# Feed-forward products of 512 columns over both operand parts, and later landings in the planner

## The chip, the cores and the metric

The kernel runs on one core of a Trainium2 chip. The metric is the device time of one execution in microseconds (us), the median of several runs. The profile and the trace are of one further execution, taken by the hardware profiler.

## The reference

The input x is 256 tokens of 1024 channels. Two blocks follow each other. The first has one recurrent mixer with a dilated attention and one feed-forward; the second has two layers, each of feed-forward, sparse-attention mixer and feed-forward, so there are five feed-forwards in all. Each of the eight sub-layers is conditioned: a vector c goes through `silu(c) @ w_ada`, which gives a shift, a scale and a gate of 1024 channels each. Cut to what matters here:

```python
def swiglu(h, w13, w2):                      # w13: 1024 x 5632, w2: 2816 x 1024
    a, b = jnp.split(h @ w13, 2, axis=-1)
    return (jax.nn.silu(a) * b) @ w2

h = rms_norm(x, g) * (1 + scale) + shift
x = x + 0.5 * gate * swiglu(h, w13, w2)
```

All values are float32, and the result is compared as float32.

## The kernel before

Activations are kept transposed, channels on the 128 partitions and the 256 tokens along the free dimension (`S` = 256), as chunks of 128 x 256. A product is one matmul with a 128 x 128 piece of the weights as stationary operand and one activation chunk as moving operand, so the output chunk is 128 x 256 and lies in PSUM.

**Two parts of each number.** TensorE takes the operands from tiles of type `fp32r`. Each operand is split into a high part (the value copied into such a tile) and a low part (the value less that copy), and `mm3` makes three products for each pair of chunks: high weights by high operand, high weights by low operand, low weights by high operand, all summed in the same PSUM region. For the weights, `load_split` loads 512 KB into a tile `raw` (128 x 1024, four row chunks of a pair of column chunks), ACT writes `hi` and DVE writes `lo` = raw - hi. For the activations the same is done once for a chunk: `hh` and `hl` are the parts of the normalised input, `fh` and `fl` (or `fg`) those of the gated hidden values.

**The feed-forward** (`ffn`) has 22 units (`NF`). A unit takes one column chunk of the left half of w13 and the matching one of the right half, 8 row chunks each. The first three units run on the input before its normalisation is known (`pair_u`, 258 columns, banks "a" and "b"). The other 19 use `pair`: both column chunks lie in one PSUM bank of the name "mm", the first in columns 0 to 255, the second in columns 256 to 511, and two such banks take turns. Then ACT makes `su` = silu of the first, DVE makes `fy` = second times `su`, and `split` makes the parts. The output product (`out_proj`) runs over 22 row chunks in four pairs of column chunks; the last pair has a bank for each chunk so that the end comes earlier. Below, the 19 units are called a feed-forward's first half, the output product its second half.

**Conditioning.** `_ada_unit` loads a row block of w_ada (`raw<-in_ada`, 128 x 1024) and reduces it against c in one DVE instruction, whose discarded full-size output is the tile `junk`. `load_split` starts such a block after a part of the weight loads (`rate` 0.55 for each load), until all are done; the results are needed sub-layers later.

**The order.** Every stretch of the kernel is recorded first: each call makes an `_Op` with an engine, a cost and a lag, and the overlaps of tiles make the edges (`_Stretch.add`, `edge`). `emit` then solves a list schedule by these costs, tries several, and issues each engine's instructions in the order of the best one; an engine works through its own in that order. All instructions have the line L725 in the profile, since one helper issues them, so they are told apart by the tiles' names. The planner's cost of a load is

```python
            if self.name == "dma":
                return rec.add(_Op("dma", emit, n / 360e3, 0.0), [out], src)
```

with no lag beyond a fixed 0.95 us from a load to the engine that reads it (`LAG`).

Of the kernel before, what the change touches and what calls it, by code (L numbers as in the profile page):

```python
# [12 lines left out]
F32 = mybir.dt.float32  # L13
# [13 lines left out]
S = 256  # L27
# [4 lines left out]
SHIFT = 2560  # L32
HP = HS = 0
EXPM05 = float(np.exp(np.float64(-0.5)))

# [580 lines left out]
class _Model:  # L618


    def __init__(self):
        self.at = {"pe": 0.0, "dve": 0.0, "act": 0.0, "pool": 0.0, "dma": 0.0}
        self.uses, self.slots = {}, {}
        self.rec = None
# [54 lines left out]
class _Engine:  # L679
# [42 lines left out]
    def record(self, op, f, a, k):  # L722
        rec = self.model.rec
        aps = [x for x in (*a, *(v for n, v in k.items() if n != "accum_out")) if _is_ap(x)]
        emit = lambda: f(*a, **k)  # L725
        if op == "dma_start":
            out = aps[0]
            src = [aps[1]] if aps[1].space == SBUF else []
            n = out.nbytes() if callable(out.nbytes) else out.nbytes
            if self.name == "dma":  # L730
                return rec.add(_Op("dma", emit, n / 360e3, 0.0), [out], src)
            return rec.add(_Op(self.name, emit, 0.06, 2.2 + n / 360e3), [out], src)
        if not aps:
            return rec.add(_Op(self.name, emit, 1.28, 0.0), [], [])
        outs = [aps[0]] + ([k["accum_out"]] if k.get("accum_out") is not None else [])
        ins = aps[1:]
        x = _Op(self.name, emit, self.time(op, aps[0], ins, k), 0.0)
        if self.name == "pe":

            x.sums = k.get("start") is False  # L740
            rows, cols = ins[0].ap[0][1], aps[0].ap[0][1]
            at = lambda a: a.offset // a.ap[0][0] // 32
            x.cols = ins[1].free_size() * rows * cols / 16384.0 * \
                (1 if ins[1].dtype == F32R else 2 if k.get("is_transpose") else 4)
            x.pas = 1 if ins[1].dtype == F32R or k.get("is_transpose") else 2
            x.d = x.hold = x.cost / x.pas
            size = lambda n: 32 if n <= 32 else 64 if n <= 64 else 128
            x.mode = size(rows), size(cols)
            if x.mode != (128, 128):
                r0, c0 = at(ins[0]), at(aps[0])  # L750
                x.subs = tuple(4 * r + c for r in range(r0, r0 + x.mode[0] // 32) for c in range(c0, c0 + x.mode[1] // 32))
                x.hold = (x.pas - 1) * x.d + 0.007
            else:
                x.hold = x.cost
        elif self.name in ("dve", "pool"):
            x.port = sum(1 for a in ins if a.space == SBUF and a.free_size() > 1) > (self.name == "dve")
        return rec.add(x, outs, ins)
# [30 lines left out]
class _Kernel:  # L788
# [90 lines left out]
    def vec(self, name, j=0, n=None):  # L879
        o, w = self.vat[name]  # L880
        return self.vect[:, o + j:o + (w if n is None else j + n)]

    def split(self, y, hi, lo):

        self.act(hi, y)
        self.tt(lo, y, hi.bitcast(F32), SUB)
# [134 lines left out]

    def mm3(self, out, wh, wl, xh, xl, first, last):
        self.mm(out, wh, xh, first, False)
        self.mm(out, wh, xl, False, False)
        self.mm(out, wl, xh, False, last)

    def pair(self, nk, H, L, tag="mm", last=False):

# [137 lines left out]

    def scaled(self, sub, pool, tag):

        self.G = [self.t(pool, [128, S], tag % j) for j in range(KC)]
        for j, g in enumerate(self.G):  # L1170
            self.act(g, self.x[j], AF.Copy, scale=self.mod(sub)[:, 8 + j:9 + j])

# [2 lines left out]
        self.chunk_hl(self.G[j], self.mod(sub), j, j >= 8)  # L1175

    def chunk_hl(self, n, m, j, pool=False):
        h = self.t(self.hp, [128, S], "hh%d" % j, F32R)
        l = self.t(self.hp, [128, S], "hl%d" % j, F32R)
        ins = self.act(h, n, AF.Identity, bias=m[:, j:j + 1])  # L1180
        if pool:
            self.nc.gpsimd.tensor_scalar(n, n, 1.0, m[:, j:j + 1], MUL, ADD)
            self.ptt(l, n, h.bitcast(F32), SUB)
        else:
            self.stt(l, n, m[:, j:j + 1], h.bitcast(F32), ADD, SUB)
        self.H.append(h)
        self.L.append(l)
        return ins
# [16 lines left out]
        while self.bg:  # L1205
            self.bg.popleft()()

    def out_proj(self, nk, H, L, sub, fpool=None):


        nc = self.nc
        m = self.mod(sub)
        nxt = sub + 1 if sub + 1 < self.n_sub else None
        if nxt is not None:
            self.operand_u(nxt)
        self.new_sum()
        f = []

        def update(j, src):
            if src is not None:  # L1220
                self.stt(self.x[j], src, m[:, 16 + j:17 + j], self.x[j], MUL, ADD)
            rec = self.model.rec
            if nxt is not None:
                rec.late = -40 / 10
                self.chunk_u(nxt, j)
            rec.late = 40 / 10
            self.add_square(self.x[j], j, KC - 4 if fpool is not None else KC - 2)
            rec.late = 0.0

        for p in range(4):  # L1230
            ps = self.pair(nk, H, L, last=p == 3)
            for c in range(2):
                j = 2 * p + c
                pc = ps[c] if p == 3 else ps[:, c * S:c * S + S]
                if fpool is None:
                    update(j, pc)
                else:
                    t = self.t(fpool, [128, S], "f%d" % j)
                    self.add_square(pc, j)
                    self.act(t, pc, AF.Copy, scale=m[:, 16 + j:17 + j])  # L1240
                    f.append(t)
        if fpool is not None:
            r = self.rstd(self.sums)
            self.behind_r = self.r_ins
            self.keep_warm(14, H[0], self.sums)
            self.new_sum()
            for j in range(KC):
                self.tt(f[j], f[j], r, MUL)
                self.tt(self.x[j], f[j], self.x[j], ADD)
                update(j, None)  # L1250


    def ffn(self, sub, n):
        tc, nc = self.tc, self.nc
        n_u = 3
        with ExitStack() as rx:
            fp, ft = (self.pool(rx, "ffn%d%d" % (n, b), b) for b in (1, 2))
            hh, hl = [], []
            pend = []

            def gated(k, y):
                h = self.t(fp, [128, S], "fh%d" % k, F32R)
                l = self.t(fp, [128, S], "fl%d" % k if k < NF - KC else "fg%d" % (k - NF + KC), F32R)
                self.split(y, h, l)
                hh.append(h)
                hl.append(l)

# [27 lines left out]
            for k in range(n_u, NF):  # L1295
                if sub == 2 and k == 8:
                    self.rope2_tables(self.pool(rx, "rt2"))
                ps = self.pair(KC, self.H, self.L)
                su = self.t(ft, [128, S], "su")
                self.act(su, ps[:, :S], AF.Silu)  # L1300
                y = self.t(ft, [128, S], "fy")
                self.tt(y, ps[:, S:], su, MUL)
                gated(k, y)
            self.use_table(LNEXP)
            self.out_proj(NF, hh, hl, sub, fp if sub < 2 else None)
            self.emit(sub + 3, rx)


    def weave(self, streams, dense=None, share=0.0):
# [82 lines left out]
    def token_loads(self, w, H, L, views, post):  # L1392
# [5 lines left out]
        def quantum(k, q):  # L1398
            def f(hi, lo):
                if k == 0:  # L1400
                    box.extend(self.psum("mm") for _ in range(2))
                ws = slice(q * w, q * w + w)
                for x, (xh, xl) in enumerate(zip(views(H[k]), views(L[k]))):
                    pv = box[x][:, :w]
                    self.mm(pv, xh, hi[:, ws], k == 0, False)
                    self.mm(pv, xl, hi[:, ws], False, False)
                    self.mm(pv, xh, lo[:, ws], False, k == KC - 1)
# [9 lines left out]
    def start(self, late):  # L1417
# [15 lines left out]
        for k in range(KC):  # L1433
# [3 lines left out]
            self.act(gs, gs, AF.Identity, scale=self.vec("g0", k, 1), bias=b1[:, k:k + 1])  # L1437
            self.act(shift, shift, AF.Identity, bias=self.vec("b0", k, 1))
            self.act(xr[k], xr[k], AF.Identity, scale=gs, bias=shift)
            h = self.t(self.hp, [128, S], "hh%d" % k, F32R)  # L1440
            l = self.t(self.hp, [128, S], "hl%d" % k, F32R)
            ins = self.act(h, xr[k])
            self.tt(l, xr[k], h.bitcast(F32), SUB)
            self.H.append(h)
            self.L.append(l)
            while k >= 6 and late:
# [18 lines left out]
    def mixer1(self, sub):  # L1465
        tc, nc, vec = self.tc, self.nc, self.vec
        with ExitStack() as cx:
# [178 lines left out]
            for n in range(4):  # L1646
                psa = self.pair(6, zh, zl)
                psb = self.pair(2, oh, ol, "a").rearrange("p (a b) -> p a b", a=2)
                for c in range(2):
# [7 lines left out]
                            psb[:, c].rearrange("p (r i) -> p i r", r=2),  # L1657
                            s2[:, 1].rearrange("p (i r) -> p i r", r=2), MUL)
                    self.tt(a1, a1, b1, ADD)
                    h = self.t(self.hp, [128, S], "hh%d" % j, F32R)  # L1660
                    l = self.t(self.hp, [128, S], "hl%d" % j, F32R)
                    self.split(a1, h, l)
                    mH.append(h)
                    mL.append(l)
            self.use_table(LNEXP)
# [511 lines left out]
    def mixer2(self, sub, l):  # L2177
        nc = self.nc
        c2 = self.c2
        with ExitStack() as cx:  # L2180
# [139 lines left out]
            oH, oL = [None] * 8, [None] * 8  # L2320

            def finished(n, po):
                oH[n] = self.t(p1, [128, S], "oh%d" % n, F32R)
                oL[n] = self.t(p1, [128, S], "ol%d" % n, F32R)
                self.act(oH[n], po[:, :S])
                self.tt(oL[n], po[:, :S], oH[n].bitcast(F32), SUB)

            def nsa(j, bank):
                gt = res["gt"]
# [138 lines left out]
```

## Time and profile before

| | |
|---|---|
| median of 3 runs | 1653.19 us |
| lowest and highest | 1648.75 and 1653.45 us |
| the profiled execution's own time | 1650.98 us |
| its span, first to last instruction | 1648.9 us |
| mean granted TensorE clock over the span | 0.992 |
| busy share of the span: PE, DVE, ACT | 96%, 75%, 58% |
| read from HBM | 356.25 MB |

PE is TensorE's matmuls, PEld its weight loads, DVE is VectorE, ACT is ScalarE, SP is SyncE, which issues all loads. Busy time is the union of an engine's instructions, and a matmul's end is modelled, so the spacing between the starts of matmuls says more than their durations. The span is the profiled execution's; 2.1 us of its own time lie around it.

### The profile page before, as it was taken

How to read it: one execution, taken by the hardware profiler on the slowest of the kernel's cores; microseconds unless marked ns; L12 is line 12 of the kernel's file. 1: busy time of each engine (PE TensorE's matmuls, PEld its weight loads, DVE VectorE, ACT ScalarE, POOL GpSimd, SP SyncE). 2: the span in 40 equal slices, each digit the busy share in tenths (PEclk: the TensorE clock that was granted, in tenths of full speed). 3: DMA queues.
4: the chain of work that ended last, by engine and by line, in shares of the span. 5: the costliest groups of instructions: out<-in, count | busy, mean ns of one | idle time of the engine just before them, and what ended most of it. 6: DMA issues, size and time to landing. Idle time of an engine off the chain costs nothing. (4 is left out here: it accounts for less than half of the span.)

```text
span 1648.9 us, 35735 instructions
## 1 busy us (share of the span) xinstructions
PE 1581.3 (96%) x14250; PEld 1495.3 (91%) x14250; DVE 1234.8 (75%) x2547; ACT 962.2 (58%) x1851; POOL 18.5 (1%) x39
## 2 busy tenths in 40 slices
PE   4999999989999899999999999999999999999998
PEld 4988888889999899999788999999999978899997
DVE  6897775687777797787869877778768887875544
ACT  5674554767444474445697744456454569874542
POOL 0010000000000000000000000000000000000001
PEclk9999999989999999999999999999999999999999
DMA  9645354465888858888524588876888753255552
GB/s 363 254 141 195 101 182 147 134 220 181 292 290 290 285 199 299 281 298 280 173 92 145 184 294 296 277 278 214 300 274 302 278 170 116 82 168 198 182 174 95
DMA packets 102696, 359.64 MB, mean 218 GB/s; under 512 B 11392, under 2 KB 13056, under 8 KB 102528
## 3 DMA queue, kind: packets, MB, share of 16 engines
q1 hardware_dynamic: 102528, 357.34, 63.6%
q8 instruction: 112, 1.84, 0.5%
q14 instruction: 56, 0.46, 0.1%
HBM read 356.25 MB, written 1.05 MB: 217 GB/s over the span
## 5 line engine op out<-in xcount | busy, mean ns | idle before, releaser
L725 DVE TENSOR_TENSOR lo<-raw,hi 128x1024 fp32r<-128x1024 f32 (+2 forms) x478 | 556.3, 1184 | 187.4 <-issue 75.9
L725 ACT ACTIVATE hi<-raw 128x1024 fp32r<-128x1024 f32 (+2 forms) x478 | 486.8, 1026 | 350.7 <-PE ps_mm L725 254.4
L725 PE MATMUL ps_mm<-hh,hi 128*128 128x256 f32 x2040 | 510.0, 286 | 19.2 <-ACT hh L725 9.2
L725 PE MATMUL ps_mm<-hl,hi 128*128 128x256 f32 x2040 | 505.2, 285 | 0.0
L725 PEld LDWEIGHTS ps_mm<-hh,hi 128*128 128x128 f32 x2040 | 387.4, 192 | 27.7 <-DVE fy L725 12.0
L725 PEld LDWEIGHTS ps_mm<-hl,hi 128*128 128x128 f32 x2040 | 387.2, 192 | 2.0 <-issue 0.8
L725 PE MATMUL ps_mm<-hh,lo 128*128 128x256 f32 x2040 | 316.7, 286 | 0.0
L725 DVE CUSTOM_DVE_ANT_0 junk<-raw,cond 128x1024 bf16<-128x1024 f32 x192 | 235.6, 1227 | 64.0 <-DMA raw<-in_ada 63.3
L725 PEld LDWEIGHTS ps_mm<-hh,lo 128*128 128x128 f32 x2040 | 275.7, 193 | 2.9 <-issue 1.1
L725 PE MATMUL ps_mm<-fh,hi 128*128 128x256 f32 x770 | 188.9, 281 | 0.0
L725 PEld LDWEIGHTS ps_mm<-fh,hi 128*128 128x128 f32 x770 | 144.5, 188 | 0.9 <-DVE fy L725 0.9
L725 PE MATMUL ps_mm<-fl,hi 128*128 128x256 f32 x490 | 120.4, 280 | 0.0
L725 PE MATMUL ps_mm<-fh,lo 128*128 128x256 f32 x770 | 115.5, 281 | 2.5 <-DVE lo L725 2.5
L725 PEld LDWEIGHTS ps_mm<-fh,lo 128*128 128x128 f32 x770 | 102.0, 188 | 2.8 <-DVE lo L725 2.8
L725 ACT ACTIVATE fh<-fy 128x256 fp32r<-128x256 f32 x110 | 44.9, 412 | 94.1 <-DVE fy L725 94.1
L725 PEld LDWEIGHTS ps_mm<-fl,hi 128*128 128x128 f32 x490 | 92.2, 188 | 0.0
L725 PE MATMUL ps_mm<-fg,hi 128*128 128x256 f32 x280 | 69.4, 281 | 0.0
L725 PE MATMUL ps_a<-UH,hi 128*128 128x258 f32 x168 | 49.4, 297 | 6.1 <-ACT UH L725 6.1
L725 PEld LDWEIGHTS ps_mm<-fg,hi 128*128 128x128 f32 x280 | 52.7, 188 | 0.0
L725 ACT ACTIVATE su<-ps_mm 128x256 f32<-128x256 f32 x95 | 35.6, 375 | 29.0 <-PE ps_mm L725 28.9
L725 ACT ACTIVATE UH<-x,mod 128x256 fp32r<-128x256 f32 x56 | 26.4, 501 | 43.6 <-DVE x L725 43.6
L725 PE MATMUL ps_a<-UL,hi 128*128 128x258 f32 x168 | 48.9, 293 | 0.0
(559 smaller groups left out, 2631.3 us busy)
## 6 DMA issues: line engine op xcount, KB each, us to landing
raw<-in_ffi SPq DMA_DIRECT2D x220, 512.0 KB, 5.4
raw<-in_ada SPq DMA_DIRECT2D x192, 512.0 KB, 5.3
raw<-in_ffo SPq DMA_DIRECT2D x100, 512.0 KB, 5.1
raw<-in_win SPq DMA_DIRECT2D x66, 512.0 KB, 4.3
raw<-in_wout SPq DMA_DIRECT2D x24, 512.0 KB, 4.1
w<-in_cw SPq DMA_DIRECT2D x16, 512.0 KB, 8.0
raw<-in_ws SPq DMA_DIRECT2D x16, 448.0 KB, 7.5
raw<-in_ffo SPq DMA_DIRECT2D x20, 256.0 KB, 4.0
```

The source lines that it names most:

```text
L725: emit = lambda: f(*a, **k)
```

## The change

Three things change in the feed-forwards. First, the high and low parts of an activation chunk share one tile of 128 x 2 x 256, high part first. `parts` makes it and returns the high part and the whole tile; `low` picks the low part out of a whole tile. Second, `pair_wide` replaces `pair` in the 19 units and in three of the four output pairs: one product of 512 columns multiplies the high weights by both parts of the operand into a bank of its own, and one of 256 columns adds low weights by high part to the bank's first half. The two column chunks now take two banks, both of one name, and the names "mm", "a" and "b" rotate. `halves` adds the bank's two halves: ACT copies the second into a tile `wa` and DVE adds the first. Third, while `late_dma` is set, the planner gives loads into tiles with rows of 1024 numbers a lag: 2.0 us for a conditioning row (group 12), 0.7 us for others. The mixers keep their products and get the shared tiles' layout; the last output pair and the first three units keep theirs too.

```diff
--- before.py
+++ after.py
@@ -32,6 +32,11 @@
+def low(x):
+
+    return x[:, 1] if len(x.shape) == 3 else x
...
@@ -728,7 +735,10 @@
             src = [aps[1]] if aps[1].space == SBUF else []
             n = out.nbytes() if callable(out.nbytes) else out.nbytes
             if self.name == "dma":
-                return rec.add(_Op("dma", emit, n / 360e3, 0.0), [out], src)
+                lag = 0.0
+                if self.model.late_dma and out.shape[-1] == D:
+                    lag = 2.0 if rec.group == 12 else 0.7
+                return rec.add(_Op("dma", emit, n / 360e3, lag), [out], src)
...
+    def halves(self, ps, pool):
+
+        t = self.t(pool, [128, S], "wa")
+        self.act(t, ps[:, S:], AF.Copy)
+        self.tt(t, ps[:, :S], t, ADD)
+        return t
...
     def mm3(self, out, wh, wl, xh, xl, first, last):
         self.mm(out, wh, xh, first, False)
-        self.mm(out, wh, xl, False, False)
+        self.mm(out, wh, low(xl), False, False)
         self.mm(out, wl, xh, False, last)
+
+    def pair_wide(self, nk, H, L):
+
+
+        tag = self.wide[0]
+        self.wide.rotate(-1)
+        ps = [self.psum(tag) for c in range(2)]
+        for r in range(0, nk, 4):
+            m = min(4, nk - r)
+            hi, lo = self.fetch()
+            for q in range(m):
+                k = r + q
+                for c in range(2):
+                    w = slice(q * 256 + c * 128, q * 256 + c * 128 + 128)
+                    self.mm(ps[c], hi[:, w], L[k].rearrange("p a b -> p (a b)"), k == 0, False)
+                    self.mm(ps[c][:, :S], lo[:, w], H[k], False, k == nk - 1)
+        return ps
+
+    def parts(self, pool, tag, t=None):
+
+        t = self.t(pool, [128, 2, S], tag, F32R) if t is None else t
+        return t[:, 0], t
...
     def scaled(self, sub, pool, tag):
 
-        self.G = [self.t(pool, [128, S], tag % j) for j in range(KC)]
+        def two(j):
+            g = self.t(pool, [128, 2, S], tag % j)
+            return g[:, 0], g[:, 1]
+
+        self.G = [g for j in range(KC // 2) for g in two(j)]
         for j, g in enumerate(self.G):
             self.act(g, self.x[j], AF.Copy, scale=self.mod(sub)[:, 8 + j:9 + j])
...
     def chunk_hl(self, n, m, j, pool=False):
-        h = self.t(self.hp, [128, S], "hh%d" % j, F32R)
-        l = self.t(self.hp, [128, S], "hl%d" % j, F32R)
+        h, l = self.parts(self.hp, "hh%d" % j)
         ins = self.act(h, n, AF.Identity, bias=m[:, j:j + 1])
         if pool:
             self.nc.gpsimd.tensor_scalar(n, n, 1.0, m[:, j:j + 1], MUL, ADD)
-            self.ptt(l, n, h.bitcast(F32), SUB)
+            self.ptt(low(l), n, h.bitcast(F32), SUB)
         else:
-            self.stt(l, n, m[:, j:j + 1], h.bitcast(F32), ADD, SUB)
+            self.stt(low(l), n, m[:, j:j + 1], h.bitcast(F32), ADD, SUB)
...
-    def out_proj(self, nk, H, L, sub, fpool=None):
+    def out_proj(self, nk, H, L, sub, fpool=None, wide=None):
...
         for p in range(4):
-            ps = self.pair(nk, H, L, last=p == 3)
+            two = wide is not None and p < 3
+            ps = self.pair_wide(nk, H, L) if two else self.pair(nk, H, L, last=p == 3)
             for c in range(2):
                 j = 2 * p + c
-                pc = ps[c] if p == 3 else ps[:, c * S:c * S + S]
+                pc = ps[c] if two or p == 3 else ps[:, c * S:c * S + S]
+                if two:
+                    pc = self.halves(pc, wide)
                 if fpool is None:
                     update(j, pc)
...
     def ffn(self, sub, n):
         tc, nc = self.tc, self.nc
         n_u = 3
+        self.model.late_dma = True
+        self.wide = deque(("mm", "a", "b"))
         with ExitStack() as rx:
...
             def gated(k, y):
-                h = self.t(fp, [128, S], "fh%d" % k, F32R)
-                l = self.t(fp, [128, S], "fl%d" % k if k < NF - KC else "fg%d" % (k - NF + KC), F32R)
-                self.split(y, h, l)
+                h, l = self.parts(fp, "fh%d" % k if k < NF - 4 else "fg%d" % (k - NF + 4))
+                self.split(y, h, low(l))
                 hh.append(h)
                 hl.append(l)
...
             for k in range(n_u, NF):
                 if sub == 2 and k == 8:
                     self.rope2_tables(self.pool(rx, "rt2"))
-                ps = self.pair(KC, self.H, self.L)
+                ps = [self.halves(p, ft) for p in self.pair_wide(KC, self.H, self.L)]
                 su = self.t(ft, [128, S], "su")
-                self.act(su, ps[:, :S], AF.Silu)
+                self.act(su, ps[0], AF.Silu)
                 y = self.t(ft, [128, S], "fy")
-                self.tt(y, ps[:, S:], su, MUL)
+                self.tt(y, ps[1], su, MUL)
                 gated(k, y)
             self.use_table(LNEXP)
-            self.out_proj(NF, hh, hl, sub, fp if sub < 2 else None)
+            self.out_proj(NF, hh, hl, sub, fp if sub < 2 else None, ft)
             self.emit(sub + 3, rx)
+        self.model.late_dma = False
...
```

## Rows read from the trace of the kernel before

**Rows 1.** The page: span, and each engine's busy us, share and instructions.

```profile
span 1648.9 us, 35735 instructions
...
PE 1581.3 (96%) x14250; PEld 1495.3 (91%) x14250; DVE 1234.8 (75%) x2547; ACT 962.2 (58%) x1851; POOL 18.5 (1%) x39
```

**Rows 2.** Busy us (count) in stretches: first halves 1 to 5; third second half.

```profile
core 0: us, PE busy (x) PEld busy (x) DVE busy (x) ACT busy (x) POOL busy (x), PEclk, DMA share, GB/s
...
385.20:500.60 115.40, 111.48 (x921) 109.90 (x919) 85.22 (x131) 57.34 (x84) 0.00 (x0) 1.00 0.77 261
...
591.40:702.60 111.20, 110.55 (x920) 109.73 (x918) 88.39 (x144) 57.52 (x85) 0.00 (x0) 1.00 0.80 275
...
932.50:1044.00 111.50, 110.60 (x919) 109.59 (x918) 86.12 (x132) 55.34 (x80) 0.00 (x0) 1.00 0.81 275
1044.00:1106.70 62.70, 62.70 (x529) 62.66 (x529) 49.58 (x78) 28.30 (x39) 0.00 (x0) 1.00 0.81 275
...
1124.70:1237.10 112.40, 110.97 (x921) 109.72 (x919) 86.74 (x136) 55.24 (x81) 0.00 (x0) 1.00 0.80 273
...
1465.60:1577.00 111.40, 110.71 (x921) 109.75 (x919) 65.26 (x94) 55.33 (x80) 0.00 (x0) 1.00 0.56 186
```

**Rows 3.** PE in order of time: start, length; a first and a second half.

```profile
1000.78 0.28 PE L725 MATMUL ps_mm<-hh,hi 128*128 128x256 f32 x1
...
1002.58 0.28 PE L725 MATMUL ps_mm<-hl,hi 128*128 128x256 f32 x1
...
719.80 0.28 PE L725 MATMUL ps_mm<-fh,hi 128*128 128x256 f32 x1
...
722.06 0.28 PE L725 MATMUL ps_mm<-fl,hi 128*128 128x256 f32 x1
```

**Rows 4.** PE in order of time: 512-column products of two mixers.

```profile
1349.04 0.39 PE L725 MATMUL ps_mm<-hi,hh 128*128 128x512 f32 x1
...
1351.80 0.39 PE L725 MATMUL ps_mm<-hi,hh 128*128 128x512 f32 x1
...
155.15 0.39 PE L725 MATMUL ps_mm<-hi,hh 128*128 128x512 f32 x1
...
155.85 0.39 PE L725 MATMUL ps_mm<-hi,hl 128*128 128x512 f32 x1
```

**Rows 5.** Groups of instructions, whole span: count | busy, mean ns | idle before.

```profile
L725 DVE CUSTOM_DVE_ANT_0 junk<-raw,cond 128x1024 bf16<-128x1024 f32 x192 | 235.6, 1227 | 64.0 <-DMA raw<-in_ada 63.3
...
L725 DVE TENSOR_TENSOR fy<-ps_mm,su 128x256 f32<-128x256 f32 x95 | 39.9, 420 | 0.9 <-ACT su L725 0.5
L725 ACT ACTIVATE su<-ps_mm 128x256 f32<-128x256 f32 x95 | 35.6, 375 | 29.0 <-PE ps_mm L725 28.9
```

**Rows 6.** DVE, then PE, in order of time, first feed-forward's first half.

```profile
409.12 1.22 DVE L725 CUSTOM_DVE_ANT_0 junk<-raw,cond 128x1024 bf16<-128x1024 f32 x1 [4.49 <-DMA raw<-in_ada]
...
411.41 0.42 DVE L725 TENSOR_TENSOR fy<-ps_mm,su 128x256 f32<-128x256 f32 x1
411.74 1.22 DVE L725 TENSOR_TENSOR lo<-raw,hi 128x1024 fp32r<-128x1024 f32 x1
...
411.88 0.39 PE L725 MATMUL ps_mm<-hh,hi 128*128 128x256 f32 x1 [1.85 <-DVE fy L725]
```

**Rows 7.** Waits: us, times, longest; first, then fourth feed-forward's first half.

```profile
DVE lo L725 <- issue: 13.6, 3, 5.1
DVE junk L725 <- DMA raw<-in_ada: 13.5, 5, 4.5
...
PE ps_mm L725 <- DVE fy L725: 3.9, 5, 1.9
...
DVE junk L725 <- DMA raw<-in_ada: 7.1, 5, 2.1
...
PE ps_mm L725 <- DVE fy L725: 1.4, 2, 0.9
```

More of the change, by code (lines that the diff above doesn't have):

```diff
@@ L621, in __init__ @@
     def __init__(self):
+        self.late_dma = False
         self.at = {"pe": 0.0, "dve": 0.0, "act": 0.0, "pool": 0.0, "dma": 0.0}
@@ L1402, in f @@
                 ws = slice(q * w, q * w + w)
-                for x, (xh, xl) in enumerate(zip(views(H[k]), views(L[k]))):
+                for x, (xh, xl) in enumerate(zip(views(H[k]), views(low(L[k])))):
                     pv = box[x][:, :w]
@@ L1439, in start @@
             self.act(xr[k], xr[k], AF.Identity, scale=gs, bias=shift)
-            h = self.t(self.hp, [128, S], "hh%d" % k, F32R)
-            l = self.t(self.hp, [128, S], "hl%d" % k, F32R)
+            h, l = self.parts(self.hp, "hh%d" % k)
             ins = self.act(h, xr[k])
-            self.tt(l, xr[k], h.bitcast(F32), SUB)
+            self.tt(low(l), xr[k], h.bitcast(F32), SUB)
             self.H.append(h)
@@ L1659, in mixer1 @@
                     self.tt(a1, a1, b1, ADD)
-                    h = self.t(self.hp, [128, S], "hh%d" % j, F32R)
-                    l = self.t(self.hp, [128, S], "hl%d" % j, F32R)
-                    self.split(a1, h, l)
+                    h, l = self.parts(self.hp, "hh%d" % j)
+                    self.split(a1, h, low(l))
                     mH.append(h)
@@ L2322, in finished @@
             def finished(n, po):
-                oH[n] = self.t(p1, [128, S], "oh%d" % n, F32R)
-                oL[n] = self.t(p1, [128, S], "ol%d" % n, F32R)
+                oH[n], oL[n] = self.parts(p1, "oh%d" % n)
                 self.act(oH[n], po[:, :S])
-                self.tt(oL[n], po[:, :S], oH[n].bitcast(F32), SUB)
+                self.tt(low(oL[n]), po[:, :S], oH[n].bitcast(F32), SUB)
             def nsa(j, bank):
```

## The prediction

> **What bounds the kernel now.** I read the page first, then the busy time of each stretch, the rows of TensorE in order of time, and the waits. The page has PE busy in 96% of the span and DVE in 75% [rows 1]. That mean says little about the change, which touches five stretches alone, so the second view cuts the span at the borders of the feed-forwards. Each has a long first half (19 gated units) and a second half (the output product). In both PE has hardly a free microsecond: 110.55 of 111.20 us in the second feed-forward's first half, 62.70 of 62.70 in the third's second half, at a granted clock of 1.00 [rows 2]. DVE is busy for 85 to 88 of about 112 us in the first halves that still reduce conditioning rows, and for 65.26 of 111.40 in the last, which has none. So PE sets the time, by the number of products times their spacing, and DVE is the one engine near enough to take its place.
>
> The spacing stands in PE's order of time. In a first half the 256-column products start every 120 ns (15 steps from 1000.78 to 1002.58), in a second half every 119 ns (19 steps from 719.80 to 722.06) [rows 3]. The feed-forwards have no 512-column product, but the mixers do: 12 steps from 1349.04 to 1351.80 are 230 ns each, 3 steps from 155.15 to 155.85 are 233 ns [rows 4].
>
> **Fewer products.** Now each weight chunk (row chunk k, column chunk c) costs three products of 256 columns: high weights by high operand, high weights by low operand, low weights by high operand. The change puts the first two into one of 512 columns. Per feed-forward that is 19 units x 8 row chunks x 2 column chunks = 304, and 3 output pairs x 22 x 2 = 132; together 436, and 2180 in all five. Each replaces 2 x 119.5 = 239 ns by 231.5 ns, the middle of the rows, and so gives 7.5 ns: 2180 x 7.5 ns = 16.4 us. The bounds are the worst and best pairing of the same rows: 2 x 119 - 233 = 5 ns, 10.9 us, and 2 x 120 - 230 = 10 ns, 21.8 us. One weight load in three goes too. I cost that at nothing, because in these stretches weight loads run beside the products (PEld 109.73 us beside PE's 110.55) [rows 2] and the spacing that I multiply already contains them.
>
> A rule speaks for less. The Trainium skill, page "TensorE: Matmul & The Clock Gate", section "Back-to-back issue gap", gives a warm gap of columns/2.4 ns plus 2.5 ns: 109.2 ns for 256 columns and 215.8 for 512. Both measured spacings are longer [rows 3, 4]; by the page, as an estimate, a merge would save 2.5 ns, 2180 of them 5.5 us, and the sum would end near 1645.5 us instead.
>
> **The sum's two halves.** High-by-low now lands in its own half of a bank, so each of the 38 + 6 output tiles per feed-forward needs one ACT copy out of PSUM and one DVE add: 220 of each. The nearest rows have the same shape and source: ACT su from PSUM 375 ns, DVE fy from PSUM and SBUF 420 ns [rows 5]. The next DVE instruction after such an fy starts 0.33 us later (411.41 to 411.74) [rows 6], so what an add takes from DVE lies between 0.33 and 0.42 us; I use 0.335 and keep 0.42 as the other end. For the second feed-forward's first half DVE then needs 88.39 + 38 x 0.335 = 101.1 us (104.4 at the other end), while PE's time falls to 111.20 - 304 x 0.0075 = 108.9 us. DVE is left with 7.8 us (4.5) where it had 22.8. The output half gets 6 adds: 49.58 + 2.5 = 52.1 of about 61.7 us, no danger. ACT goes from 57.52 by 38 x 0.375 = 14.3 to 71.8 of 108.9 us, no danger. So 220 adds (74 to 92 us) and 220 copies (82 us) cost nothing while PE covers them; every microsecond that DVE needs over those 7.8 comes back as PE time in that stretch.
>
> What eats the 7.8 us is waiting. DVE takes instructions in order, so while it waits for one late conditioning row (junk), the low weight parts (lo) and gated values (fy) queued behind it wait as well. The trace shows the whole sequence: junk waits 4.49 us until 409.12, fy behind it comes at 411.41, and PE, which wants that value, stood still for 1.85 us until 411.88 [rows 6]. Such waits add up to 13.5 us in the first feed-forward's first half and 7.1 in the fourth's [rows 7]. The larger idle time, 13.6 us before lo in three pieces, is another kind: PE does not stop through it, so I read it as DVE being ahead and take it as room to spare.
>
> **Later landings.** The planner now counts on 2.0 us more for a conditioning row and 0.7 us for a full weight row. No instruction is added; the order on all queues changes, with SP asked earlier for these rows relative to their use and DVE reaching their reductions later. What that can give back is PE's wait behind DVE: 3.9 us in the first half of the first feed-forward, 1.4 in the fourth's [rows 7], and by these two I allow 1 us for each of the others; 0 to 8 us. I take 4. Against it I put 4 us of new waits, 1 us in each of the four first halves in which DVE is left with less than 8 us; the ends are 0 and, if the waits for rows stay as they are, about 12.
>
> **What is moved or longer.** High and low operand parts share a tile, so a 512-column product waits for ACT's and DVE's part, where the first product had needed ACT's only. It matters at the first unit alone, later ones have theirs long before. A unit's result comes 0.375 + 0.42 = 0.8 us later. What hides it is the other pairs: three PSUM pairs rotate now ("mm", "a", "b") where two buffers of one name did, and at the change to the output product the last gated chunk is needed only after about 20 of 22 row chunks, some 14 us later. If that cover were gone, 0.8 us per feed-forward, 4 us in all. The mixers' layout changes, their work does not: 0.
>
> **Sum.** Profiled execution 1650.98 (span 1648.9 and 2.1 around it) - 16.4 - 4 + 4 = 1634.6 us. The median of the three runs, 1653.19, is 2.2 above that execution, and the lowest, 1648.75, is 2.2 below; I say 1636.
>
> **Rivals.** (1) DVE becomes the bound. For: 92.8% of the new PE time is planned work (95.9% at 0.42 us an add), and each wait in that in-order queue delays lo. Against: the waits for rows that the trace shows, 7.1 us, would still just fit, and the new lag is meant for them. It decides when DVE's waits in a first half pass 7.8 us; at 4.1 us more, 12 us of waits in each of four, the whole 16.4 us is gone, and at 20 us the time is 1650.98 - 16.4 + 4 x 12.2 = 1683; I take the middle, 16 us of waits: 1650.98 - 16.4 + 4 x 8.2 = 1667. Chance 0.12, the other side of no change.
>
> (2) The merge gives nothing, because the products cost by their columns: one of 512 would take what two of 256 take, 239 ns. Then only the later landings act, 0 to 8 us gained less 4 lost: about 1649. Rows 4 speak against it, in stretches with small products between; the cited page would put it at the edge of this case. Chance 0.07.
>
> (3) Half: through the smaller reserve DVE takes back 8 to 16 of the 16.4 us, 2 to 4 us in each of four first halves: 1636 + 8 to 1636 + 16, 1644 to 1652. Chance 0.12, of which 0.05 ends within 0.3%.
>
> (4) More than the sum: 10 ns a merge and all waits behind conditioning rows gone, 1650.98 - 21.8 - 8 = 1621 at the best; 1621 to 1628. Chance 0.07.
>
> The forecast itself, 1628 to 1643, has 0.62.
>
> **How the numbers follow.** About 0.3%, 5 us, is what a measurement of this kernel can tell from no change. Faster: 0.62 + 0.07 + 0.07 = 0.76. Within: 0.07 + 0.05 = 0.12. Slower: 0.12. The range leaves out the slower rival and the far end of (4): 1625 to 1655.
>
> **What would show it.** Right: MATMUL counts fall by 2180 from 14250 [rows 1] to about 12070; 512-column products in the feed-forwards start about 231 ns before their followers; a first half takes 108 to 110 us instead of 111 to 115; DVE has about 101 us busy there; waits for conditioning rows well under the 63.3 us in all that they are now [rows 5]. Wrong: a PE that idles in first halves before lo or fy, DVE over 95% busy there, first halves that are longer than before, or a spacing of 239 ns for the merged product. The prediction fails first if DVE's order, laid out anew by the planner, leaves PE waiting more than a microsecond or two in each first half.

## The result, and the profile after

The changed kernel takes 1626.93 us (median of 4 runs, 1621.52 to 1631.68), the kernel before 1652.58 us beside it (4 runs, 1648.75 to 1653.45): a ratio of 0.9857, interval 0.9828 to 0.9886, so 1.4% faster. The prediction was 1636 us in 1625 to 1655. The profiled execution took 1631.68 us, its span is 1629.9 us, and its mean granted clock is 0.987 where before had 0.992.

The page after, against [rows 1]: the 2180 products are gone, and the additions stand on DVE and ACT.

```profile
span 1629.9 us, 32029 instructions
...
PE 1562.4 (96%) x12070; PEld 1388.2 (85%) x12070; DVE 1308.1 (80%) x2767; ACT 1031.2 (63%) x2071; POOL 17.9 (1%) x39
```

PE's busy share stayed at 96%, so the share says nothing of the gain. The stretches do. These are the windows that answer to [rows 2]: first halves 1 to 3, one second half, first halves 4 and 5.

```profile
388.90:494.90 106.00, 106.00 (x610) 93.24 (x609) 95.11 (x163) 67.92 (x116) 0.00 (x0) 1.00 0.82 276
583.60:689.50 105.90, 105.90 (x610) 93.17 (x609) 96.25 (x175) 68.50 (x122) 0.00 (x0) 1.00 0.78 265
...
920.60:1026.50 105.90, 105.90 (x609) 93.10 (x608) 89.84 (x155) 64.80 (x113) 0.00 (x0) 1.00 0.79 266
1026.60:1088.30 61.70, 61.70 (x398) 55.93 (x397) 55.02 (x91) 31.04 (x48) 0.00 (x0) 1.00 0.82 284
...
1107.00:1213.00 106.00, 106.00 (x610) 93.17 (x609) 90.68 (x160) 65.78 (x115) 0.00 (x0) 1.00 0.80 264
...
1452.70:1558.20 105.50, 105.50 (x608) 92.80 (x607) 74.23 (x125) 65.29 (x113) 0.00 (x0) 1.00 0.59 190
```

The first two columns are equal in each row: PE has no idle time left in any of these stretches, and the five first halves, which differed (111.20 to 115.40 us), are now 105.5 to 106.0. DVE is at 96.25 of 105.90 us in the fullest.

PE in order of time, in the second feed-forward's first half:

```profile
614.29 2.00 PE L732 MATMUL ps_mm<-hh,hi 128*128 128x512 f32 x8
616.13 2.03 PE L732 MATMUL ps_b<-hh,hi 128*128 128x512 f32 x8
618.00 1.32 PE L732 MATMUL ps_mm<-hh,hi 128*128 128x512 f32 x5
```

Eight products from 614.29 to 616.13 are 230 ns each, the next eight 234. Two of DVE's adds, and what follows them:

```profile
605.15 0.75 DVE L732 TENSOR_TENSOR wa<-ps_b,wa 128x256 f32<-128x256 f32 x2
605.82 1.21 DVE L732 TENSOR_TENSOR lo<-raw,hi 128x1024 fp32r<-128x1024 f32 x1
```

Two adds take 0.67 us until the next instruction starts, 0.335 each. And the group that answers to the first of [rows 5]:

```profile
L732 DVE CUSTOM_DVE_ANT_0 junk<-raw,cond 128x1024 bf16<-128x1024 f32 x192 | 235.0, 1224 | 12.7 <-DMA raw<-in_ada 11.8
```

DVE's waits for conditioning rows fell from 63.3 to 11.8 us.

**A ledger for all runs.** I cut each profile at the borders of the five feed-forwards (from the first 258-column product to the last of the output product) and added the five stretches. These are the sum lines of those windows, before and then after:

```profile
sum 972.30, PE 962.23 PEld 954.84 DVE 708.97 ACT 506.95 POOL 4.79; mean PE 192.45 PEld 190.97 DVE 141.79 ACT 101.39 POOL 0.96
```

```profile
sum 937.20, PE 937.12 PEld 842.53 DVE 776.80 ACT 574.85 POOL 5.08; mean PE 187.42 PEld 168.51 DVE 155.36 ACT 114.97 POOL 1.02
```

So the feed-forwards gained 35.1 us and the span only 19.0 (1648.9 to 1629.9). Outside the feed-forwards 16.1 us were lost, 10.8 of them in the last mixer, which went from 148.0 to 158.8 us. Two questions follow: what the 35.1 us consist of, and why stretches without one changed instruction became slower.

### The profile page after: what moved, and what is told of

Same layout as the page of the kernel before. It is cut to its first block, busy times and chain, and to the rows that moved or that the text cites. A ratio compares the mean times of both kernels' runs of the same rounds, so it can differ in the third digit from the quotient of the medians.

```text
span 1629.9 us, 32029 instructions
## 1 busy us (share of the span) xinstructions
PE 1562.4 (96%) x12070; PEld 1388.2 (85%) x12070; DVE 1308.1 (80%) x2767; ACT 1031.2 (63%) x2071; POOL 17.9 (1%) x39
## 4 chain that ended last, share of the span: by engine, by line
PE 68%; DVE 5%; ACT 4%; DMA 1%; issue 1%; DVEq 0%; SPq 0%; ACTq 0%
PE ps_mm L732 25%; PE ps_a L732 22%; PE ps_b L732 19%; PE ps_c L732 2%; DMA raw<-in_win 1%; DVE lo L732 1%; ACT P1a L732 1%; ACT hi L732 1%; ACT P0a L732 1%; DVE zb L732 0%; DVE rt L732 0%; DVE junk L732 0%; DVE hh L732 0%; ACT P1b L732 0%; DVE f L732 0%
## 5 line engine op out<-in xcount | busy, mean ns | idle before, releaser
L732 PE MATMUL ps_mm<-hh,hi 128*128 128x256 f32 (+1 forms) x1600 | 312.0, 329 | 13.5 <-ACT hh L732 9.0
L732 PEld LDWEIGHTS ps_mm<-hh,hi 128*128 128x128 f32 x1600 | 248.3, 193 | 40.3 <-ACT hh L732 9.9
L732 DVE CUSTOM_DVE_ANT_0 junk<-raw,cond 128x1024 bf16<-128x1024 f32 x192 | 235.0, 1224 | 12.7 <-DMA raw<-in_ada 11.8
L732 PE MATMUL ps_mm<-hh,lo 128*128 128x256 f32 x1080 | 173.7, 286 | 0.0
L732 PEld LDWEIGHTS ps_mm<-hh,lo 128*128 128x128 f32 x1080 | 149.4, 191 | 5.0 <-issue 0.5
L732 PE MATMUL ps_a<-hh,hi 128*128 128x512 f32 (+1 forms) x560 | 137.1, 378 | 0.0
L732 PE MATMUL ps_b<-hh,hi 128*128 128x512 f32 (+1 forms) x544 | 130.8, 379 | 0.0
L732 PEld LDWEIGHTS ps_a<-hh,hi 128*128 128x128 f32 x560 | 101.0, 190 | 18.5
L732 PEld LDWEIGHTS ps_b<-hh,hi 128*128 128x128 f32 x544 | 96.5, 189 | 17.5
L732 PE MATMUL ps_mm<-fh,hi 128*128 128x512 f32 (+1 forms) x360 | 82.5, 337 | 0.0
L732 PEld LDWEIGHTS ps_mm<-fh,hi 128*128 128x128 f32 x360 | 60.3, 188 | 6.4
```

## The experiments

The theory after the result: (a) the merge gives about 17 us, (b) the other 18 are PE's waits in the feed-forwards, and (c) the loss outside comes with the order that the planner writes. The rival to (b) was that the later landings alone had removed those waits, the rival to (c) that it was chance. "Feed" below is the sum of the five stretches as above.

**The changed kernel again** (e1_again and e10_changed, each on another chip; no edit).

> The changed kernel once more, as the control on this chip. Its first four runs fell into two groups, 1631.6 and 1621.9 us, and the profiled one (1631.7) had the granted clock at half for 13.6 us in the last mixer. If the clock there makes the two groups, a profile of a run near 1622 shows the last mixer at about 147 us instead of 156.5 and no half clock in its middle, and the five first halves unchanged at 529 us together. If it is something else, the mixer is as long as before in the faster runs too.

> The changed kernel a third time, on one chip with the run before and the two behind. By its eight executions so far: 1621 to 1634 us with a median near 1628, feed-forwards 937 to 939 us in the profile, the last mixer near 159 us with TensorE at half clock for some 10 us of it.

Measured: 1628.63 us (1625.80 to 1633.73), ratio 0.9873 [0.9855, 0.9891], and 1625.35 (1623.92 to 1632.13), 0.9860 [0.9837, 0.9883]. Feed 938.8 and 937.3. The last mixer took 159.1 and 157.7 us, so its loss is no chance. The time up to the first feed-forward was 365.1 and 360.7 us, and 367.1 in the first profile, with one and the same order; that part of the loss belongs to the execution and not to the change. What e1 asked stays open: neither profiled execution (1633.73 and 1626.76 us) was one near 1622 us, so nothing shows what parts the faster executions from the others.

**Part (b), one cure at a time.** In the kernel before, all pairs of a unit's sums share the two buffers of one PSUM name. e2_narrow_rotate lets them rotate over three names and changes nothing else; e3_lag_only adds the later landings alone; e8_narrow_rotate_lag has both. None has the merge.

```
-                ps = self.pair(KC, self.H, self.L)
+                ps = self.pair(KC, self.H, self.L, self.turn())     # e2, e8: "mm", "a", "b" in turn
...
+                    lag = 2.0 if rec.group == 12 else 0.7            # e3, e8: as in the change
+                return rec.add(_Op("dma", emit, n / 360e3, lag), [out], src)
```

> The kernel before, with its three products of 256 columns, without later landings; only its pairs take their PSUM banks from the names mm, a and b in turn instead of from mm alone. Theory B (PE's waits in the first halves are for a PSUM bank that fy has not yet read out): the waits go, the five first halves together fall from 561.9 us to 912 x 0.1193 = 109 us each, 544 to 548, and the time by 14 to 18 us to about 1636. Theory L (they come from conditioning rows that land late and hold up DVE): nothing goes, 558 to 562 us, time about 1652.

> The kernel before with the later landings in the planner alone (2.0 us for conditioning rows, 0.7 us for weight rows, in the feed-forwards). Theory L: DVE's waits for conditioning rows fall from 63.3 us to about 12, the five first halves from 561.9 to 544 to 548 us, time about 1636. Theory B: those waits of DVE fall too, but the first halves stay at 555 to 560 us, since PE still waits for banks; time 1645 to 1650. My prediction's terms were 4 us for this.

> The kernel before with both cures, rotating bank names and later landings, and no merging. If the two remove the same waits, as the two runs with one of them suggest (five feed-forwards 12.6 and 13.0 us shorter), the feed-forwards take about 955 us, 17 to 18 us less than before, and the time is 1634 to 1640. If they add up, 947 us or less. What then is left to the changed kernel's 937 us is the merge alone, 2180 x 8 ns = 17.4 us.

Measured: e2 1640.59 us (1636.31 to 1644.72), 0.9947 [0.9930, 0.9963]; e3 1641.09 (1639.52 to 1641.87), 0.9953 [0.9938, 0.9968]; e8 1631.93 (1628.73 to 1634.63), 0.9885 [0.9862, 0.9908]. Their sum lines, in this order:

```profile
sum 959.70, PE 955.55 PEld 952.67 DVE 707.43 ACT 503.28 POOL 4.54; mean PE 191.11 PEld 190.53 DVE 141.49 ACT 100.66 POOL 0.91
```

```profile
sum 959.30, PE 957.19 PEld 952.77 DVE 712.00 ACT 508.01 POOL 4.79; mean PE 191.44 PEld 190.56 DVE 142.40 ACT 101.60 POOL 0.96
```

```profile
sum 954.80, PE 953.68 PEld 952.07 DVE 711.03 ACT 503.00 POOL 4.54; mean PE 190.74 PEld 190.41 DVE 142.21 ACT 100.60 POOL 0.91
```

The names alone give 12.6 us, the landings alone 13.0, and both 17.5: they cure largely the same waits. Neither theory came out whole. e2 gained nearly what theory B says in the feed-forwards, but its median is only 8.7 us below the kernel before on the same chip (1649.28); e3, for which theory B expected 1645 to 1650 us, gained as much as e2. e8 came out at the 955 us of its first case, and its time 2 us below the 1634 to 1640 given with it. What the waits were, e2 shows. DVE's waits in its first feed-forward's first half, and the group over the whole span:

```profile
DVE junk L725 <- DMA raw<-in_ada: 12.5, 5, 3.8
...
L725 DVE CUSTOM_DVE_ANT_0 junk<-raw,cond 128x1024 bf16<-128x1024 f32 x192 | 235.2, 1225 | 86.5 <-DMA raw<-in_ada 86.2
```

DVE stands there almost as long as before (13.5 us [rows 7]), and over the span its waits for rows are longer, 86.2 us against 63.3 [rows 5]. Yet PE has no wait in that half, where it had 3.9 us behind fy. PE had not waited for the value: no product of that half reads fy. It waited for the bank out of which the delayed fy had still to read. With six banks in place of two, the delay does not reach PE.

**The landings under the wide product** (e4_wide_no_lag): the change without its later landings.

```
-                    lag = 2.0 if rec.group == 12 else 0.7
+                    lag = 0.0
```

> The changed kernel with a lag of 0 in the planner. Theory B: the five first halves stay at 529 to 533 us, since three pairs of banks carry PE over DVE's waits; time within 4 us of the changed kernel in the same clock state. Theory L: DVE, 91% busy there, waits 5 to 13 us for rows in each of four first halves, PE follows, and they take 540 us or more; time 10 us or more above the changed kernel.

Measured: 1636.99 us (1633.52 to 1637.88), 0.9926 [0.9909, 0.9942]; feed 950.1, 12.9 more than the change. The time lies between the two theories, 8.4 us above the changed kernel on the same chip (1628.63). Of the 12.9 us, 10.2 stand in the first two feed-forwards (194.80 and 193.50 us where the change takes 188.70 and 189.40), not in four. The waits in the first one's first half:

```profile
PE ps_a L732 <- DVE lo L732: 2.6, 1, 2.6
PE ps_b L732 <- DVE lo L732: 0.7, 1, 0.7
...
DVE junk L732 <- DMA raw<-in_ada: 15.4, 4, 4.9
```

DVE, then PE in order of time, in the same stretch:

```profile
478.11 1.23 DVE L732 CUSTOM_DVE_ANT_0 junk<-raw,cond 128x1024 bf16<-128x1024 f32 x1 [4.92 <-DMA raw<-in_ada]
479.26 1.22 DVE L732 TENSOR_TENSOR lo<-raw,hi 128x1024 fp32r<-128x1024 f32 x1
...
480.54 1.98 PE L732 MATMUL ps_a<-hh,lo 128*128 128x256 f32 x8 [2.55 <-DVE lo L732]
```

This is the first rival's mechanism: a conditioning row comes 4.92 us late, the low weight part queued behind it is late, and PE stands 2.55 us, now truly for a value. After that wait the granted clock was at half for 3.4 us. So the changed kernel needs the later landings beside its rotating banks, where e2 without them is only 4.9 us behind e8. Whether that comes from the adds on DVE, or from the banks, of which a unit now takes two, so that three units are in flight and not six, no run separates.

**Part (a), the merge alone** (e5_two_256): the same banks, copies, adds and landings, but the 512 columns made by two products into the halves of the bank.

```
-                    self.mm(ps[c], hi[:, w], L[k].rearrange("p a b -> p (a b)"), k == 0, False)
+                    self.mm(ps[c][:, :S], hi[:, w], H[k], k == 0, False)
+                    self.mm(ps[c][:, S:], hi[:, w], low(L[k]), False, False)
```

> The changed kernel with each 512-column product made as two of 256 columns with the same stationary weights, into the same two halves of the same bank; banks, adds, layout and landings stay. Theory M (a merge gives the difference of spacings, 2 x 119 - 230 = 8 ns): 2180 x 8 ns = 17.4 us slower than the changed kernel, each first half 106.0 + 304 x 0.008 = 108.4 us, each second half 61.7 + 132 x 0.008 = 62.8 us. The page's rule (2.5 ns each): 5.5 us slower, first halves 106.8 us. Theory C (cost by columns): no difference.

Measured: 1633.38 us (1631.78 to 1635.80), 0.9896 [0.9875, 0.9917]. Its sum line:

```profile
sum 954.30, PE 953.85 PEld 952.26 DVE 780.12 ACT 574.03 POOL 5.09; mean PE 190.77 PEld 190.45 DVE 156.02 ACT 114.81 POOL 1.02
```

954.30 - 937.20 = 17.1 us for 2180 merges, 7.8 ns each, as theory M expects. A product undone is also a weight load more (14250 of each in e5, 12070 in the change), so the 7.8 ns are for both together. The total differs by about 6 us only, mostly because this kernel's last mixer took 150.3 us. The feed is also within half a microsecond of e8's 954.80, which has no copies and no adds: 440 instructions on ACT and DVE cost nothing there.

**How near DVE was** (e7_add_twice): each add is made twice, the first time into a tile that nobody reads.

```
+        u = self.t(pool, [128, S], "wb")
+        self.tt(u, ps[:, :S], t, ADD)
         self.tt(t, ps[:, :S], t, ADD)
```

> The changed kernel with the DVE add of each output tile made twice, the first time into a tile that nobody reads (220 more adds). My prediction says that DVE has room in a first half of 106 us: it is busy 96 us in the second feed-forward's (with 16 conditioning rows). 38 x 0.335 = 12.7 us more make about 109 there: the first four first halves become 2 to 5 us longer each, the fifth (74 us busy) and all second halves do not, 8 to 20 us in all. If the reserve is larger than I read it (conditioning rows can move into second halves and mixers), nothing changes within 3 us. If a busy DVE hurts earlier, through waits behind it, more than 20 us.

Measured: 1639.19 us (1637.44 to 1640.87), 0.9930 [0.9909, 0.9950]; feed 952.7, 15.5 more than the change. The windows: first half 1, then the first three units of the second feed-forward and the second's first half.

```profile
384.00:490.00 106.00, 106.00 (x609) 92.86 (x608) 104.47 (x187) 65.76 (x116) 0.00 (x0) 1.00 0.79 266
...
556.70:585.60 28.90, 23.23 (x154) 22.41 (x155) 24.21 (x52) 22.77 (x44) 0.00 (x0) 0.83 0.70 241
...
585.70:691.60 105.90, 105.90 (x610) 93.10 (x609) 104.09 (x199) 62.86 (x111) 0.00 (x0) 1.00 0.80 270
```

The first halves kept their 106.0 us with DVE busy for 104.47 of them. The loss stands elsewhere: 28.90 us in the first three units, where the changed kernel needs 21.50:

```profile
562.00:583.50 21.50, 21.47 (x154) 20.91 (x155) 19.36 (x47) 18.86 (x38) 0.00 (x0) 0.92 0.76 273
```

SP's queue just before that stretch of e7 says why:

```profile
543.59 21.30 SPq L732 DMA_DIRECT2D raw<-in_ada  x6
564.95 2.59 SPq L732 DMA_DIRECT2D raw<-in_ffi  x5
```

Six loads of conditioning rows hold the queue for 21.30 us, since the rows have two buffers and a load waits until a reduction has freed one. The weight rows behind them are issued only at 564.95, and PE stands 4.7 us for the first (ACT hi). The fourth feed-forward repeats it (25.00 for 18.50 us). A DVE that falls behind is paid for one stage later, through SP's queue. The 15.5 us lie in the expected 8 to 20, but not in the first halves, where I expected them: the mechanism of that expectation was wrong.

**Part (c), the order.** e6_two_names and e9_two_names (the same kernel on two chips) rotate two names instead of three; e11_cond_only counts on later landings for conditioning rows alone; e12_other_noise gives the planner's trial orders another random seed.

```
-        self.wide = deque(("mm", "a", "b"))
+        self.wide = deque(("mm", "a"))                            # e6, e9
...
-                    lag = 2.0 if rec.group == 12 else 0.7
+                    lag = 2.0 if rec.group == 12 else 0.0         # e11
...
-        rng = np.random.RandomState(0)
+        rng = np.random.RandomState(1)                            # e12
```

> The changed kernel with its pairs of banks from the names mm and a alone, so that two pairs can be in flight as before and not three; landings stay late. If the later landings alone keep DVE from holding PE up, the five first halves stay at 529 to 532 us. If the third pair of banks is what carries PE over DVE's fuller queue, PE waits for banks again and they take 535 us or more.

> The kernel with two bank names again, now timed on one chip beside the changed kernel. Its feed-forwards took as long as the changed kernel's (939.6 against 937.0 us), everything outside them 16 us less (677.1 against 692.9). If that is a property of the order that the planner found, it repeats: 1614 to 1622 us, outside part 675 to 681 us. If it was that chip's luck, it takes 1625 to 1633 as the changed kernel does.

> The changed kernel with the lag on conditioning rows alone (2.0 us) and none on weight rows. If the conditioning rows are what held DVE up, the feed-forwards stay at 937 to 940 us. If late weight rows matter too (ACT's hi waits for them), they take 942 to 950 us, towards the 950.1 us without any lag.

> The changed kernel with another seed for the noise by which the planner scores its schedules: the same instructions in another order. If what lies outside the feed-forwards is set by the order that the planner happens on, the feed-forwards stay at 936 to 941 us and the rest lands anywhere between 671 and 693 us. If the changed layout or the feed-forwards' bank names make the mixers slower, the rest stays at 690 us or more.

Measured: e6 1617.93 us (1613.71 to 1619.43), 0.9794 [0.9767, 0.9822]; e9 1617.75 (1614.74 to 1620.79), 0.9807 [0.9789, 0.9826]; e11 1625.74 (1624.21 to 1628.15), 0.9857 [0.9841, 0.9874]; e12 1627.81 (1623.79 to 1630.59), 0.9867 [0.9846, 0.9887]. Feeds 939.5, 938.7, 937.9 and 936.9. e6 is at most 2.3 us behind the change in the feed-forwards, so with the landings late a third pair of banks gives little. e9 repeats e6: outside the feed-forwards it takes 680.3 us, within the 675 to 681 expected. The planner came to the same order with the other seed, so e12 is one more run of the changed kernel and its question stays unanswered. e11 says that the 0.7 us for weight rows makes no difference that shows, as the first of its two cases has it. Two names are the best version of the study: on one chip 1617.75 us beside 1625.35 for the change, and in the profiles all of it lies outside the feed-forwards. The shared tiles' layout is not what makes the last mixer slow: e5, e6 and e9 have it too, and take 149.0 to 150.3 us there.

What the change loses there, the start of the last mixer shows first. SP's queue of the changed kernel there (the fourth feed-forward ends at 1274.8), and PE's and ACT's waits in the mixer's first 20 us with their window:

```profile
1263.74 14.30 SPq L732 DMA_DIRECT2D raw<-in_ada  x5
1278.14 2.28 SPq L732 DMA_DIRECT2D raw<-in_win  x4
```

```profile
ACT hi L732 <- DMA raw<-in_win: 6.2, 4, 5.5
...
PE ps_a L732 <- ACT hi L732: 4.8, 1, 4.8
```

```profile
1274.80:1294.80 20.00, 15.16 (x109) 14.79 (x108) 12.81 (x26) 11.54 (x22) 0.00 (x0) 0.91 0.84 302
```

And e9, whose fourth feed-forward ends at 1272.1:

```profile
1261.20 4.68 SPq L732 DMA_DIRECT2D raw<-in_ada  x2
1265.93 2.03 SPq L732 DMA_DIRECT2D raw<-in_win  x4
```

```profile
1272.10:1292.10 20.00, 20.00 (x155) 19.00 (x153) 17.50 (x46) 15.04 (x30) 0.00 (x0) 1.00 0.90 336
```

It is e7's sequence at another border. In the changed kernel three conditioning reductions are left over when the feed-forward ends; five loads of such rows hold SP's queue for 14.30 us; the mixer's weight rows (in_win) are issued 3.3 us after the feed-forward's end; PE idles 4.8 us, and then the granted clock is at half for 3.4 us. In e9 the four rows are issued 6.2 us before the end, and PE does 155 products in 20 us instead of 109. The table has this time for all profiles (when the block of three or four in_win loads is issued, against the end of the fourth feed-forward, and the reductions that start after it):

| profile | in_win issued | reductions left | last mixer, us |
|---|---|---|---|
| before | 5.4 us earlier | 0 | 148.0 |
| e8 / e3 | 10.2 / 10.2 earlier | 0 / 0 | 149.0 / 151.9 |
| e6 / e9 | 6.2 / 6.2 earlier | 0 / 0 | 149.0 / 149.7 |
| e2 / e4 | 5.5 / 5.2 earlier | 0 / 0 | 151.3 / 150.1 |
| e5 | 2.2 earlier | 1 | 150.3 |
| e11 | 2.4 later | 3 | 156.2 |
| after / e1 / e10 / e12 | 3.3 / 3.3 / 3.4 / 3.5 later | 3 / 3 / 3 / 3 | 158.8 / 159.1 / 157.7 / 158.9 |
| e7 | 4.8 later | 4 | 154.2 |

The two groups do not overlap: at most 151.9 us with the rows issued in time, at least 154.2 without. Within the second group the time of issue does not set the length, though: e7, the latest, has the shortest mixer.

The count of products that PE has begun tells where the time goes. Against e9 the changed kernel is 7.0 us behind after 155 products and 9.1 at the mixer's end, e10 6.7 and 8.0: most of that difference arises at the start. e11 loses only 2.1 us there and 4.6 more by product 300, where PE waits 3.0 us for ACT (hs) and the granted clock is at half for 6.8 us; so its long mixer is not mainly this sequence. Against the kernel before, the change is 7.3 us behind at product 820 and 11.2 at product 850. Between them the granted clock falls to half for 10.2 us (from 1399.5); in the kernel before it does not fall in that stretch. The change and then the kernel before, at about the same products:

```profile
1394.80:1404.80 10.00, 7.81 (x40) 6.09 (x39) 8.00 (x24) 8.82 (x32) 0.00 (x0) 0.73 0.16 53
```

```profile
1409.60:1419.60 10.00, 8.60 (x70) 7.41 (x71) 9.03 (x45) 9.83 (x34) 0.00 (x0) 1.00 0.12 44
```

So this late fall, which e9 has too (10.2 us from 1388.7), is no part of what separates the change from e9, but it goes with about 4 of the 10.8 us against before. No kernel was built that moves the in_win loads alone: the sequence and the delay at the start are shown, that the queue is the cause of the whole loss is not.

## Why the prediction was right, and where its sizes were off

- **Fewer products, 16.4 us (10.9 to 21.8).** Right: 17.1 us, 7.8 ns a merge. The spacing of 230 and 119 ns carried over from the mixers and the second halves [rows 3, 4]. The Trainium skill, page "TensorE: Matmul & The Clock Gate", section "Back-to-back issue gap", would have made it an estimate of 5.5 us. I left out that this section of the Trainium skill gives the formula for an isolated product, and about 131 ns at 512 columns for a stream of weight loads and products. The measurement decides against both here: 230 to 234 ns, and 17.1 us. Rival (2), no gain from the merge, falls by e5.
- **440 added instructions at nothing.** Right: e5 and e8 have the same feed, 954.30 and 954.80. The add's 0.335 us was met by the pair shown; by the feeds of e5 and e8 (780.12 and 711.03 us of DVE) 220 adds took 0.314 each. DVE's 101 us came out at 96.25, mainly since 16 reductions fell into that half instead of 19.
- **Rival (1), DVE the bound.** Not in the changed kernel, whose first halves have no wait of PE. The mechanism was real: e4 shows it as soon as the landings are taken back. Its price was put in the wrong place: e7 shows that even a DVE at 104.47 of 106.00 us does not slow that half; what it leaves undone delays the next stage's weights.
- **Later landings give back 0 to 8, take 4; new waits 4.** The term was mis-sized: waits removed 17.5 us (e8), new waits nothing, and the first halves took 105.5 to 106.0 us where I had said 108 to 110. I had read the wait in [rows 6] as one for fy's value and costed the rotating names as cover only. It was a wait for the bank, so a second cure, worth 12.6 us alone (e2), stood unpriced. I also counted only the idle times behind fy. Over the whole feed-forwards PE's time without a product was 972.30 - 962.23 = 10.1 us, readable in the windows of before. Nearly all of the rest is the same stalls, which busy time hides in part because a product's end is modelled. Counted by starts at full clock, the products of the 19 units and of the output lost 18.1 us before, in 67 steps longer than 0.13 us (beyond 0.119 each), and 1.6 us in 6 such steps in e8.
- **"The mixers' layout changes, their work does not: 0."** Wrong in its conclusion. Their work is the same, but the queue ahead of them is not: the last mixer lost 10.8 us, some 7 of them from its start. I had written that the order on all queues changes and did not follow SP's over the border of the stage.
- **The total** came out within its range by luck in part, because two errors had opposite signs: 18.7 us more gained inside the feed-forwards than the 16.4 forecast (35.1), 16.1 lost outside, for which nothing was forecast.

The small rest is open: 3.5 us up to the first feed-forward are within what the same order shows from one execution to another (360.7 to 367.1), 1.4 in the first layer's mixer were not followed. Open as well is why the planner leaves three reductions over with three names and none with two.

## What to carry to other kernels

When PE waits for an engine, ask whether the product reads that engine's value or overwrites the bank that it still reads: the second is cured by more names in rotation, without making anyone faster. Measure a change by stretches, because a planner that lays out its order anew can give back in untouched stages what the changed stage gains. Look at each stage border for loads that wait for a buffer ahead of the next stage's first weights in an in-order queue.

## What was not expected of the hardware

- DVE at 98.6% busy (104.47 of 106.00 us, e7) did not slow PE beside it at all.
- A single short wait of PE was followed by a granted clock at half: for 3.4 us after 2.55 us of waiting in e4 (from 480.7) and after 4.8 us at the start of the last mixer (from 1286.9), and, later in that mixer, for 10.2 us shortly after 2.19 us (from 1399.5). The 1.85 us before [rows 6] were followed by none.
- One load that waits for its buffer holds all loads behind it on SP's queue: six issues took 21.30 us in e7, where a single one shows 0.33 us.
